# Value products moved beside the next half's scores, two-bank PSUM tiles, the norm without GpSimd arithmetic, y transposes in pairs

## The chip, the cores and the metric

The kernel runs on one core of one Trainium2 chip. The metric is the device time of one launch in microseconds, the median of three runs. A core has a tensor engine (PE, with its weight loads shown as PEld), a vector engine (DVE), a scalar engine (ACT), a GpSimd engine (POOL) and a sync engine (SP) that issues most loads. Each executes its own instructions in order; between engines there are semaphores.

## The reference, cut to what matters

One layer for 256 prompt frames and 64 sample frames (320 columns in all, `T`), model width 2048:

```python
h = rmsnorm(x, norm_pre[l])
proj = jnp.einsum('bsd,de->bse', h, w_in[l])          # 2048 x 15392 weights
# four mixers: A stick-breaking, B chunk-band, C differential, D latent (low rank KV, rotary key)
gated = outs * jax.nn.silu(gate_in)
y_branch = jnp.einsum('bsnc,ncd->bsnd', gated, w_branch[l])
y = jnp.einsum('bsd,de->bse', jnp.sum(sigmoid(merge_in) * y_branch, axis=2), w_out[l])
x = x + rmsnorm(y, norm_post[l])
```

Each mixer is scores (q times k), a softmax or stick-breaking weight, and value products (weights times v). Keys, values and the latent cache are outputs too.

## The kernel before

All weight products keep features on the partitions and the 320 frames in the columns. A weight block of 1024 columns of SBUF is a **unit** (512 KB as a rule). A unit is loaded by SP into `raw` (4 buffers), split into a high part `whi` on ACT (L190) and a low part `wlo` on DVE (L191), 4 buffers each, and multiplied in three products per 128x128 block (L195 to L197: hi by hi, hi by lo, lo by hi). A unit has 24 products of 320 columns; four units in a row make a group that accumulates in a PSUM tile `pm` of two banks. There are two `pm` tiles by turns; the one not in use is `spare_pm()`. The main loop (L1240 on) walks over the units. One turn of it is a **slot**: it emits the load of unit i+3, the split of unit i+3, then background work, then the products of unit i.

**The start.** Units 0 to 7 are the D input projection (`d_units`, products on L910), each of two 128-row chunks k of x. For each k, `first_split` emits on ACT the cast `xhi` (L1177) and the cast `whi` (L175), on DVE `xlo` (L1180) and `wlo` (L178). Between them the table `early` places the norm's squares and sums: of the first four chunks on POOL (L1188), of the rest on ACT (L1184), with the folding sums on POOL in slot 1 (L1192) and on DVE in slots 5 and 6 (L1192). POOL also scales the rotary key weights `wkr` (L1195). Ahead of the last chunk, k=15, `x_rms` needs the folded sum: six tiny products (L1201). After k=15, `krope_mm` runs 32 products of 32 array columns (L789), four side by side.

**The attention.** The heads are cut into eight halves, in the order A0, D0, D1, A1, B0, B1, C0, C1. Each half is two generators (p=0 and p=1) run in step by `pair`; `heavy` runs one half at a time from slot 33 on. A generator yields the number of slots to wait, and with a second number says that it needs the spare `pm` tile. Its stages in fp32 on PE are the scores (L496, L513; D: L489, L490, L510; A: L602, L606, L607), the transposes of the weights (L458 to L460; C: L540 to L544) or A's running sums (L644 to L647), and the value products `pv64` (L409; C: L549 to L552). p=0 takes the spare `pm` tile for scores and transposes, p=1 takes three one-bank tiles from `att()` (four buffers in all). `v_prep`, a light generator two slots after the value group, transposes v (L700, L704), and ACT copies it out (L706, L707).

**The end.** For each of seven groups of the output projection, `out_post` scales the block into `yg`, and a light generator one slot later transposes it (L1073, L1077) and ACT copies it out.

Of the kernel before, what the change touches and what calls it, by code (L numbers as in the profile page):

```python
# [16 lines left out]
D = 2048  # L17
# [45 lines left out]
def hybrid_streaming_kernel(ctx, tc, ins, outs):  # L63
# [44 lines left out]
    def spare_pm():  # L108

        return psm.tile([128, 2, 512], F32, name="sp", tag=f"pm{turn[0] ^ 1}", bufs=1)  # L110

    def att():
        return psa.tile([128, 512], F32, name="att", tag="att", bufs=4)

# [7 lines left out]
    wkr = ppool.tile([128, KC, 32], F32, name="wkr")  # L122
    nrm = cpool.tile([128, 24], F32, name="nrm")
    npost = nrm[:, 0:16]
# [119 lines left out]

    def pair(*gens):

        live = [dict(gen=g, due=0, bar=None) for g in gens]
        while live:  # L250
            go = True
            while go:
                go = False
                for e in list(live):
                    if e["bar"] is None and e["due"] <= slot[0]:
                        try:
                            w = next(e["gen"])
                        except StopIteration:
                            live.remove(e)
# [3 lines left out]
                if live and all(e["bar"] and e["due"] <= slot[0] for e in live):  # L263
                    if live[0]["bar"][1] and not spare_ok(live[0]["bar"][1]):
                        break
                    for e in live:
                        e["bar"] = None
                    go = True
            if live:
                yield 1  # L270

# [3 lines left out]

    light, heavy = Queue(), Queue()

# [3 lines left out]
    def run_background():  # L281
        for e in list(later):
            if e[0] <= slot[0]:
                later.remove(e)
                e[1]()
        step(light)
        if slot[0] >= M["last_q"]:
            step(heavy, 1)

# [156 lines left out]
    def transposes_pt(z, p):  # L446
        p1 = R["p1"]
        zt = p1.tile([128, 1024], F32, name="zt", tag="t1", bufs=2)
        if p == 0:
            sp = spare_pm()  # L450
            tps = [sp[:, 0], sp[:, 1]]
            ts = sp[:, :, 384:512]
# [12 lines left out]

    def attn_softmax(kind, n, hf, p, q, k, v, bias_heads=None):
# [4 lines left out]
        if bias_heads is not None:  # L471
            bp, bsamp = load_bias(bias_heads)
            bias = [bp[:, 0], bp[:, 1 if len(bias_heads) > 1 else 0]]
        else:
            bias = [R["mdz"]] * 2
            bsamp = R["mdz"][:, 0:192]
        z = p1.tile([128, 1024], F32, name="z", tag="t0", bufs=2)
        mx = p1.tile([128, 16], F32, name="mx", tag="mx", bufs=4)
        st = p1.tile([128, 16], F32, name="st", tag="st", bufs=4)
        yield 0, 1 if kind == "C" else 2  # L480
        if p == 0:
            sp = spare_pm()
            S = [sp[:, 0], sp[:, 1]]
        else:
            S = [att(), att()]
        if kind == "D":
# [12 lines left out]

        if p == 0:  # L500
            SSp, zs, cuts = sp[:, :, 384:480], z[:, 768:960].rearrange("p (a c) -> p a c", a=2), 2
            bsamp = bsamp.rearrange("p (a c) -> p a c", a=2)
        else:
            SSp, zs, cuts = att()[:, 0:192], z[:, 768:960], 1
        for c in range(cuts):
            n_k = 192 // cuts
            to, kc = SSp[:, c] if cuts > 1 else SSp, slice(256 + c * n_k, 256 + c * n_k + n_k)
            if kind == "D":
# [9 lines left out]
        if kind != "C":  # L518
# [26 lines left out]
        copy_on(1, zt[:, 768:1024], tp[:, 0:256])  # L545
        yield 2, 0
        o = att()
# [38 lines left out]
    def attn_stick(n, hf, p, q, k, v):  # L586
        p1 = R["p1"]
        t0 = p1.tile([128, 1024], F32, name="a0", tag="t0", bufs=2)
        t1 = p1.tile([128, 1024], F32, name="a1", tag="t1", bufs=2)
        t2 = p1.tile([128, 1024], F32, name="a2", tag="t2", bufs=2)  # L590
        yield 0, 2
        if p == 0:
            sp = spare_pm()
            S = [sp[:, 0], sp[:, 1], sp[:, :, 384:512]]
        else:
            S = [att(), att(), None]

# [5 lines left out]
        yield 0, 0  # L603
        if p:
            S[2] = att()[:, 0:256].rearrange("p (a c) -> p a c", a=2)
        nc.tensor.matmul(S[2][:, 0], k[:, p, 256:384], qblk(q, p), start=True, stop=True)  # L606
# [46 lines left out]
        mask(t1)  # L653
        yield 2, 0
        both = t1[:, 0:512].rearrange("p (b j c) -> p j b c", b=2, j=2)
# [4 lines left out]
    def half_branch(kind, n, hf, col):  # L660
# [23 lines left out]
        def post_v(ps):  # L684
# [6 lines left out]
            nc.gpsimd.dma_start(v[:, 2, :], CV[kind][:, hf * 256:hf * 256 + 256])  # L691
            light.append(v_prep(vt))

        def v_prep(vt):
            v = H["v"]
            yield 2
            tp = att()
# [16 lines left out]
            defer(store)  # L714
            if kind == "A":
# [125 lines left out]
    def q_unit(u0):  # L841
# [34 lines left out]
        def post_nope():  # L876
            ps, g = box["ps"], u0 - 1
            q = M["q", g]
            for j in range(2):
                nc.scalar.activation(q[0:64, j:4:2, :], ps[64 * j:64 * j + 64, :, :T], AF.Copy)  # L880
            heavy.append(pair(*(attn_softmax("D", 3, g, p % 2, q, M["k", p], M["v", g])
                                for p in (2 * g, 2 * g + 1))))

# [168 lines left out]
    def out_post(e, n):  # L1052

        def post(ps):
# [13 lines left out]

            def tr():
                for t in range(2):  # L1070
                    tp = att()
                    for i in range(n):
                        nc.tensor.transpose(tp[:, i * 128:(i + 1) * 128], yg[:, i, t * 128:(t + 1) * 128], ident)  # L1073
                    nc.scalar.activation(E["y"][:, t, e * 128:(e + n) * 128], tp[:, 0:n * 128], AF.Copy)
                tp = att()
# [3 lines left out]
                nc.scalar.activation(E["ys"][r:r + 64, c * 128:(c + n) * 128], tp[0:64, 0:n * 128], AF.Copy)  # L1079
            def gen():  # L1080
                yield
                tr()
            light.append(gen())
        return post
# [86 lines left out]
    for i in range(NRAW):  # L1171
        first_load(i)

    TN = ((0, 128), (1, 128), (2, 64))
# [10 lines left out]

    def x_square_pool(c):
        x = xf[:, 4 * c:4 * c + 4, :T]
        nc.gpsimd.tensor_tensor(xsq[:, 4 * c:4 * c + 4, :], x, x, op=OP.mult)  # L1188

    def x_sum(a, n, c, on=nc.vector):  # L1190

        on.tensor_tensor(xsq[:, a:a + n, :], xsq[:, a:a + n, :], xsq[:, c:c + n, :], op=OP.add)  # L1192
# [14 lines left out]
    def x_rbc():  # L1207
        tp = M["rms"][:, 64:64 + T]
        for t, n in TN:
# [33 lines left out]
    for i, u in enumerate(units):  # L1243
# [7 lines left out]
        if i + AHEAD < FIRST:  # L1251
            first_split(i + AHEAD)
            if i == 0:
                first_load(FIRST - 1)
                nc.sync.dma_start(cp, ins["cp"])
                nc.sync.dma_start(wkr, ins["w_kr"])
                nc.sync.dma_start(nrm, ins["nrm"])
        elif i + AHEAD < len(units):
# [69 lines left out]
```

## Time and profile before

| | us |
|---|---|
| median of three runs | 1176.95 (1176.75 to 1177.08) |
| the profiled execution | 1178.38 |
| its span | 1176.5 |
| PE busy | 1166.4 |
| DVE busy | 613.7 |
| ACT busy | 502.4 |
| POOL busy | 70.4 |

The profiled execution is 1.43 above the median, and 1.88 of its time lies outside the span. Line 4 of the page gives the chain of work that ended last: PE 96% of the span, of which L195 to L197 are 88 points. In views of PE a product's start-to-start distance is its cost; the duration printed for it is longer, since products are pipelined. A row with "xN" merges N products; an fp32 product is recorded as two, a transpose as one.

### The profile page before, as it was taken

To read this page: it belongs to the slowest core of one execution; us is meant where nothing else is said; L and a number is where in the kernel's file an instruction comes from. 1 tells how busy PE (TensorE), PEld (TensorE's weight loads), DVE (VectorE), ACT (ScalarE), POOL (GpSimd) and SP (SyncE) were. 2 spreads that over 40 slices of the span, in tenths; PEclk is the share of its full clock that TensorE was granted. 3 is DMA by queue.
4 is the path that set the end of the run, shared out by engine and by line. 5 is a ranking of instruction groups with operands and counts; after the bars stand their busy time and mean duration, and the time that the engine had idled before them with its cause. 6 is when DMAs were issued, how large, how long until landed. Compare 5 with 4: busy or idle time off the path is not lost.

```text
span 1176.5 us, 19590 instructions
## 1 busy us (share of the span) xinstructions
PE 1166.4 (99%) x8139; PEld 1150.9 (98%) x8139; DVE 613.7 (52%) x849; ACT 502.4 (43%) x723; POOL 70.4 (6%) x129
## 2 busy tenths in 40 slices
PE   9999999999999999999999999999999999999997
PEld 8899999999999999999999999999999999999997
DVE  8565375555754545657444454454444454444444
ACT  7344663446444456535333333333333333334442
POOL 3311100002022010000000000000000000020000
PEclk9999999999999999999999999999999999999999
DMA  8755545445455554545554555555555555566442
GB/s 283 241 183 165 147 130 160 137 137 160 139 151 151 163 153 119 161 144 144 151 155 143 154 144 151 156 149 144 160 145 144 161 144 147 158 193 188 144 125 90
DMA packets 171512, 182.71 MB, mean 155 GB/s; under 512 B 7132, under 2 KB 165200, under 8 KB 171008
## 3 DMA queue, kind: packets, MB, share of 16 engines
q1 hardware_dynamic: 167552, 172.97, 50.1%
q0 software_dynamic: 2656, 5.32, 1.7%
q10 hardware_dynamic: 1216, 3.18, 0.8%
q8 instruction: 64, 1.05, 0.4%
q14 instruction: 24, 0.20, 0.0%
HBM read 174.56 MB, written 9.39 MB: 156 GB/s over the span
## 4 chain that ended last, share of the span: by engine, by line
PE 96%; DVE 1%; DMA 1%; ACT 1%; issue 0%; SPq 0%; DVEq 0%
PE pm L195 30%; PE pm L196 29%; PE pm L197 29%; PE att L409 1%; DMA raw<-in_w_in 1%; PE pm L1108 0%; DVE wlo L178 0%; PE pm L1110 0%; PE pm L1109 0%; PE att L644 0%; PE sp L496 0%; PE att L1073 0%; DVE xsq L1192 0%; DVE xlo L1180 0%; PE att L789 0%
## 5 line engine op out<-in xcount | busy, mean ns | idle before, releaser
L191 DVE TENSOR_TENSOR wlo<-raw,whi 128x1024 fp32r<-128x1024 f32 x301 | 365.6, 1220 | 450.4 <-ACT whi L190 448.5
L195 PE MATMUL pm<-xhi,whi 128*128 128x320 f32 x1856 | 577.5, 311 | 0.0
L197 PE MATMUL pm<-xhi,wlo 128*128 128x320 f32 x1856 | 574.1, 309 | 0.0
L196 PE MATMUL pm<-xlo,whi 128*128 128x320 f32 x1856 | 574.0, 309 | 0.0
L190 ACT ACTIVATE whi<-raw 128x1024 fp32r<-128x1024 f32 x301 | 314.7, 1052 | 410.1 <-PE pm L196 330.2
L195 PEld LDWEIGHTS pm<-xhi,whi 128*128 128x128 f32 x1856 | 348.6, 188 | 2.3 <-issue 1.7
L196 PEld LDWEIGHTS pm<-xlo,whi 128*128 128x128 f32 x1856 | 348.6, 188 | 0.2
L197 PEld LDWEIGHTS pm<-xhi,wlo 128*128 128x128 f32 x1856 | 348.5, 188 | 0.0
L197 PE MATMUL pm<-ghi,wlo 128*128 128x320 f32 x256 | 79.2, 309 | 0.0
L196 PE MATMUL pm<-glo,whi 128*128 128x320 f32 x256 | 79.2, 309 | 0.0
L195 PE MATMUL pm<-ghi,whi 128*128 128x320 f32 x256 | 79.2, 309 | 0.0
L962 ACT ACTIVATE sg<-sg 128x640 f32<-128x640 f32 x32 | 23.6, 738 | 112.4 <-DVE sg L151 112.4
L195 PE MATMUL pm<-yhi,whi 128*128 128x320 f32 x224 | 69.8, 312 | 0.0
L197 PE MATMUL pm<-yhi,wlo 128*128 128x320 f32 x224 | 69.3, 309 | 0.0
L196 PE MATMUL pm<-ylo,whi 128*128 128x320 f32 x224 | 69.2, 309 | 0.0
L151 DVE TENSOR_TENSOR sg<-pm,rbc 128x640 f32<-128x640 f32 x40 | 32.9, 823 | 44.5 <-PE pm L197 44.5
L196 PEld LDWEIGHTS pm<-glo,whi 128*128 128x128 f32 x256 | 48.1, 188 | 0.0
L195 PEld LDWEIGHTS pm<-ghi,whi 128*128 128x128 f32 x256 | 48.1, 188 | 0.0
L197 PEld LDWEIGHTS pm<-ghi,wlo 128*128 128x128 f32 x256 | 48.1, 188 | 0.0
L196 PEld LDWEIGHTS pm<-ylo,whi 128*128 128x128 f32 x224 | 42.1, 188 | 0.0
L195 PEld LDWEIGHTS pm<-yhi,whi 128*128 128x128 f32 x224 | 42.1, 188 | 0.0
L197 PEld LDWEIGHTS pm<-yhi,wlo 128*128 128x128 f32 x224 | 42.1, 188 | 0.0
(337 smaller groups left out, 889.1 us busy)
## 6 DMA issues: line engine op xcount, KB each, us to landing
raw<-in_w_in SPq DMA_DIRECT2D x237, 512.0 KB, 3.8
raw<-in_w_branch SPq DMA_DIRECT2D x32, 512.0 KB, 3.6
raw<-in_w_out SPq DMA_DIRECT2D x32, 512.0 KB, 3.8
xrp<-in_x_prompt SPq DMA_DIRECT2D x1, 2048.0 KB, 8.4
out_xp<-ytp SPq DMA_DIRECT2D x8, 256.0 KB, 2.1
xf<-in_x_t SPq DMA_DIRECT2D x5, 321.0 KB, 6.3
scr<-in_bb ACTq DMA_DIRECT2D x1, 1536.0 KB, 9.1
bp<-scr POOLq DMA_DIRECT2D x12, 128.0 KB, 2.4
```

The source lines that it names most:

```text
L151: nc.vector.tensor_tensor(out, ps, rb(n, i, rows, cols), op=OP.mult)
L190: nc.scalar.activation(h, raw, AF.Copy)
L191: nc.vector.tensor_tensor(l, raw, h.bitcast(F32), op=OP.subtract)
L195: nc.tensor.matmul(out, wh, xh, start=first, stop=False)
L196: nc.tensor.matmul(out, wh, xl, start=False, stop=False)
L197: nc.tensor.matmul(out, wl, xh, start=False, stop=last)
L409: nc.tensor.matmul(o[64 * j:64 * j + 64, a:b], v[:, blk, vc + 64 * j:vc + 64 * j + 64], z[j][blk], start=first, stop=not first)
L962: nc.scalar.activation(s, s, AF.Sigmoid)
```

## The change

- `att2()` gives a PSUM tile of two banks (two buffers); `att()` hands out halves of such a tile. p=1 takes an `att2()` tile with p=0's layout: one tile for scores and transposes, the sample scores in two products of 96 columns where p=1 had one of 192.
- `pair` becomes the class `Pair`. Up to two halves run at once. A half that stands before its value products ("pv") waits until the next half stands before its scores ("qk"); then one slot holds the next half's `v_prep`, the earlier half's value products and the next half's scores. After 10 slots of waiting, and for C1, the value products go alone. `v_prep` is no light generator any more, except for A0.
- The squares of x are all on ACT (slots 1, 3, 4, 5), the sums all on DVE (slots 3 to 6). `wkr` is scaled on DVE in slot 2, by 16 columns that `nrm` now carries; `nrm` and `wkr` are loaded behind the loads of unit 3, not behind those of unit 7.
- The y transposes of two groups are done in one slot, and those of the two prompt blocks share one copy.

```diff
+    def att2():
+        half.clear()
+        return psa.tile([128, 2, 512], F32, name="att", tag="att", bufs=2)
     def att():
-        return psa.tile([128, 512], F32, name="att", tag="att", bufs=4)
+        if not half:
+            t = att2()
+            half.extend((t[:, 1], t[:, 0]))
+        return half.pop()
...
+    WAIT = 10
+    class Pair:
+        def run(self, before=None):
+            if before and not before.scored:
+                return
...
+                    if self.at("pv") and not (self.joined or self.last or
+                                              slot[0] - max(e["due"] for e in self.live) >= WAIT):
+                        return
+                    if self.at("qk"):
+                        if before and not (before.at("pv") or before.joined or before.through):
+                            return
+                        if self.front:
+                            self.front()
+                        if before and before.at("pv"):
+                            before.joined = True
+                            before.run()
+                        self.scored = True
...
         if slot[0] >= M["last_q"]:
-            step(heavy, 1)
+            for h in range(min(2, len(heavy))):
+                heavy[h].run(heavy[0] if h else None)
+            while heavy and heavy[0].through:
+                heavy.pop(0)
...
     def transposes_pt(z, p):
-        if p == 0:
-            sp = spare_pm()
...
-        else:
-            tps = [att(), att()]
-            ts = att()[:, 0:256].rearrange("p (a c) -> p a c", a=2)
+        sp = att2() if p else spare_pm()
+        tps = [sp[:, 0], sp[:, 1]]
+        ts = sp[:, :, 384:512]
...
+        yield 0, 1 if kind == "C" else 2, "qk"
...
-        yield 0, 1 if kind == "C" else 2
-        if p == 0:
-            sp = spare_pm()
-            S = [sp[:, 0], sp[:, 1]]
-        else:
-            S = [att(), att()]
+        sp = att2() if p else spare_pm()
+        S = [sp[:, 0], sp[:, 1]]
...
-            SSp, zs, cuts = att()[:, 0:192], z[:, 768:960], 1
...
+        for c in range(2):
+            to, kc = SSp[:, c], slice(256 + c * 96, 352 + c * 96)
...
-            yield 2, 0
+            yield 2, 0, "pv"
             pv64(...)
...
-            light.append(v_prep(vt))
+            if kind == "A" and hf == 0:
+                light.append(v_early(vt))
+            else:
+                attend(3, lambda: v_prep(vt))
...
-            heavy.append(pair(*gens))
+            heavy.append(Pair(gens, front, after, kind == "C" and hf == 1))
...
             def tr():
+                tp = att().rearrange("p (t c) -> p t c", t=2)
                 for t in range(2):
-                    tp = att()
...
-            light.append(gen())
+            E.setdefault("tr", []).append(tr)
+            if len(E["tr"]) == 2 or e == 12:
+                light.append(gen(E.pop("tr")))
...
     for i in range(NRAW):
         first_load(i)
+    nc.sync.dma_start(nrm, ins["nrm"])
+    nc.sync.dma_start(wkr, ins["w_kr"])
...
     def kr_scale():
-        nc.gpsimd.tensor_tensor(wkr, wkr, xf[:, :, T:T + 1].to_broadcast([128, KC, 32]), op=OP.mult)
+        nc.vector.tensor_tensor(wkr, wkr, nrm[:, 24:40].rearrange("p (k o) -> p k o", o=1).to_broadcast([128, KC, 32]),
+                                op=OP.mult)
...
-    early = {0: [lambda: x_square_pool(0)],
-             1: [lambda: x_square(1)] + [lambda n=n: x_sum(0, n, n, nc.gpsimd) for n in (4, 2, 1)],
-             3: [lambda: x_square(2)],
-             5: [lambda: x_square(3), lambda: x_sum(8, 4, 12)],
-             6: [lambda: x_sum(8, 2, 10), lambda: x_sum(8, 1, 9), lambda: x_sum(0, 1, 8)]}
-    early[4] = [kr_scale]
+    early = {1: [lambda: x_square(0)],
+             2: [kr_scale],
+             3: [lambda: x_square(1), lambda: x_sum(0, 4, 4)],
+             4: [lambda: x_square(2), lambda: x_sum(0, 4, 8)],
+             5: [lambda: x_square(3), lambda: x_sum(0, 4, 12)],
+             6: [lambda: x_sum(0, 2, 2), lambda: x_sum(0, 1, 1)]}
```

## Rows read from the trace of the kernel before

**Rows 1.** The page, part 1: busy us (share of the span) and instructions.

```profile
PE 1166.4 (99%) x8139; PEld 1150.9 (98%) x8139; DVE 613.7 (52%) x849; ACT 502.4 (43%) x723; POOL 70.4 (6%) x129
```

**Rows 2.** Waits of PE, whole run: us in total, times, longest.

```profile
PE pm L910 <- DVE wlo L178: 1.2, 1, 1.2
PE att L1201 <- DVE xsq L1192: 1.1, 1, 1.1
```

**Rows 3.** Timeline of PE at 9 us: start us, duration us, instruction, [idle before, releaser].

```profile
8.76 0.31 PE L910 MATMUL pm<-xhi,whi 128*128 128x320 f32 x1
8.91 0.31 PE L910 MATMUL pm<-xlo,whi 128*128 128x320 f32 x1
10.38 0.41 PE L910 MATMUL pm<-xhi,wlo 128*128 128x320 f32 x1 [1.16 <-DVE wlo L178]
```

**Rows 4.** Timeline of DVE in the first 35 us.

```profile
7.54 2.78 DVE L178 TENSOR_TENSOR wlo<-raw,whi 128x512 fp32r<-128x512 f32 x1
10.25 0.54 DVE L1180 SCALAR_TENSOR_TENSOR xlo<-xf,xhi 128x320 fp32r<-128x320 f32 x1
10.71 0.68 DVE L178 TENSOR_TENSOR wlo<-raw,whi 128x512 fp32r<-128x512 f32 x1
...
16.01 3.00 DVE L1180 SCALAR_TENSOR_TENSOR xlo<-xf,xhi 128x320 fp32r<-128x320 f32 x1 [0.37 <-ACT xhi L1177]
...
29.88 1.48 DVE L1192 TENSOR_TENSOR xsq<-xsq 128x1280 f32<-128x1280 f32 x1
...
32.42 1.93 DVE L1192 TENSOR_TENSOR xsq<-xsq 128x640 f32<-128x640 f32 x3
```

**Rows 5.** Timeline of POOL in the first 35 us.

```profile
7.45 2.33 POOL L1188 TENSOR_TENSOR xsq<-xf 128x1280 f32<-128x1280 f32 x1 [6.47 <-DMA xf<-in_x_t]
15.68 6.05 POOL L1192 TENSOR_TENSOR xsq<-xsq 128x1280 f32<-128x1280 f32 x3 [5.90 <-ACT xsq L1184]
```

**Rows 6.** Timeline of PE at the norm, 34 to 37 us.

```profile
34.40 0.81 PE L1201 MATMUL att<-ones,xsq 128*128 128x2 f32 x6 [1.06 <-DVE xsq L1192]
...
36.12 0.47 PE L910 MATMUL att<-xhi,whi 128*128 128x320 f32 x1
36.39 0.47 PE L910 MATMUL att<-xlo,whi 128*128 128x320 f32 x1
```

**Rows 7.** Line L789 in two windows: us, PE, PEld busy (count), PEclk, DMA.

```profile
37.85:39.45 1.60, 1.59 (x12) 0.59 (x16) 0.50 0.94 229
39.45:40.95 1.50, 1.50 (x24) 0.51 (x16) 0.98 0.76 257
```

**Rows 8.** Timeline of PE, slot 79: v transposes and value products in one block.

```profile
320.93 0.60 PE L700 MATMUL att<-cp,vt 128*128 128x128 f32 x4
321.36 0.38 PE L704 MATMUL att<-cp,vt 128*64 128x128 f32 x2
321.67 1.99 PE L409 MATMUL att<-a,v 128*64 128x256 f32 x32
323.59 0.42 PE L195 MATMUL pm<-xhi,whi 128*128 128x320 f32 x1
323.84 0.31 PE L196 MATMUL pm<-xlo,whi 128*128 128x320 f32 x1
```

**Rows 9.** Timeline of PE, slot 82: the scores of B0 in a block of their own.

```profile
334.11 0.31 PE L197 MATMUL pm<-xhi,wlo 128*128 128x320 f32 x1
334.35 0.93 PE L496 MATMUL sp<-k,q 64*128 64x128 f32 x8
...
335.86 0.69 PE L513 MATMUL sp<-k,q 128*128 128x96 f32 x4
336.38 0.52 PE L513 MATMUL att<-k,q 128*128 128x192 f32 x2
336.60 0.44 PE L195 MATMUL pm<-xhi,whi 128*128 128x320 f32 x1
```

**Rows 10.** Timeline of ACT beside the block of slot 79.

```profile
322.65 0.46 ACT L707 ACTIVATE v<-att,rstat 64x256 f32<-64x256 f32 x1
```

More of the change, by code (lines that the diff above doesn't have):

```diff
@@ L110, in spare_pm @@
         return psm.tile([128, 2, 512], F32, name="sp", tag=f"pm{turn[0] ^ 1}", bufs=1)
+    half = []
+    def att2():
+        half.clear()
+        return psa.tile([128, 2, 512], F32, name="att", tag="att", bufs=2)
     def att():
-        return psa.tile([128, 512], F32, name="att", tag="att", bufs=4)
+        if not half:
+            t = att2()
+            half.extend((t[:, 1], t[:, 0]))
+        return half.pop()
     ppool_ctx = ExitStack()
@@ L122, in hybrid_streaming_kernel @@
     wkr = ppool.tile([128, KC, 32], F32, name="wkr")
-    nrm = cpool.tile([128, 24], F32, name="nrm")
+    nrm = cpool.tile([128, 40], F32, name="nrm")
     npost = nrm[:, 0:16]
@@ L243, in spare_ok, with __init__, at @@
         return slot[0] >= len(units) or 0 < units[slot[0]].get("left", 0) <= most
-    def pair(*gens):
-        live = [dict(gen=g, due=0, bar=None) for g in gens]
-        while live:
+    WAIT = 10
+    class Pair:
+        def __init__(self, gens, front=None, after=0, last=False):
+            self.live = [dict(gen=g, due=slot[0] + after, bar=None) for g in gens]
+            self.front, self.last, self.scored, self.joined = front, last, False, False
+        def at(self, stage):
+            return all(e["bar"] and e["due"] <= slot[0] and e["bar"][2:] == (stage,) for e in self.live)
+        def run(self, before=None):
+            if before and not before.scored:
+                return
             go = True
@@ L253, in pair @@
                 go = False
-                for e in list(live):
+                for e in list(self.live):
                     if e["bar"] is None and e["due"] <= slot[0]:
@@ L258, in pair @@
                         except StopIteration:
-                            live.remove(e)
+                            self.live.remove(e)
                             continue
@@ L262, in pair, with through @@
                         e["due"] = slot[0] + w
[L263 to L266, printed above, removed]
+                if self.live and all(e["bar"] and e["due"] <= slot[0] for e in self.live):
+                    if self.live[0]["bar"][1] and not spare_ok(self.live[0]["bar"][1]):
+                        return
[4 more added lines that the diff above has]
+                        if before and not (before.at("pv") or before.joined or before.through):
+                            return
+                        if self.front:
[4 more added lines that the diff above has]
+                        self.scored = True
+                    if self.at("pv"):
+                        self.joined = True
+                    for e in self.live:
                         e["bar"] = None
                     go = True
-            if live:
-                yield 1
+        @property
+        def through(self):
+            return not self.live
     class Queue(list):
@@ L274, in append @@
             super().append([g, 0])
-    light, heavy = Queue(), Queue()
+    light, heavy = Queue(), []
     def defer(fn, n=2):
@@ L498, in attn_softmax @@
         yield 0, 0
[L500 to L503, printed above, removed]
-            SSp, zs, cuts = att()[:, 0:192], z[:, 768:960], 1
-        for c in range(cuts):
-            n_k = 192 // cuts
-            to, kc = SSp[:, c] if cuts > 1 else SSp, slice(256 + c * n_k, 256 + c * n_k + n_k)
+        SSp, zs = sp[:, :, 384:480], z[:, 768:960].rearrange("p (a c) -> p a c", a=2)
+        bsamp = bsamp.rearrange("p (a c) -> p a c", a=2)
+        for c in range(2):
+            to, kc = SSp[:, c], slice(256 + c * 96, 352 + c * 96)
             if kind == "D":
@@ L545, in attn_softmax @@
         copy_on(1, zt[:, 768:1024], tp[:, 0:256])
-        yield 2, 0
+        yield 2, 0, "pv"
         o = att()
@@ L587, in attn_stick @@
         p1 = R["p1"]
+        yield 0, 2, "qk"
         t0 = p1.tile([128, 1024], F32, name="a0", tag="t0", bufs=2)
@@ L590, in attn_stick @@
         t2 = p1.tile([128, 1024], F32, name="a2", tag="t2", bufs=2)
[L591 to L596, printed above, removed]
+        sp = att2() if p else spare_pm()
+        S = [sp[:, 0], sp[:, 1], sp[:, :, 384:512]]
         for kb, a, b in ((0, 0, 256), (128, 256, 384)):
@@ L603, in attn_stick @@
         yield 0, 0
-        if p:
-            S[2] = att()[:, 0:256].rearrange("p (a c) -> p a c", a=2)
         nc.tensor.matmul(S[2][:, 0], k[:, p, 256:384], qblk(q, p), start=True, stop=True)
@@ L653, in attn_stick @@
         mask(t1)
-        yield 2, 0
+        yield 2, 0, "pv"
         both = t1[:, 0:512].rearrange("p (b j c) -> p j b c", b=2, j=2)
@@ L691, in post_v, with v_early @@
             nc.gpsimd.dma_start(v[:, 2, :], CV[kind][:, hf * 256:hf * 256 + 256])
-            light.append(v_prep(vt))
+            if kind == "A" and hf == 0:
+                light.append(v_early(vt))
+            else:
+                attend(3, lambda: v_prep(vt))
+        def v_early(vt):
+            yield 2
+            v_prep(vt)
+            attend(1, None)
         def v_prep(vt):
             v = H["v"]
-            yield 2
             tp = att()
@@ L714, in v_prep, with attend @@
             defer(store)
+        def attend(after, front):
+            v = H["v"]
             if kind == "A":
@@ L880, in post_nope @@
                 nc.scalar.activation(q[0:64, j:4:2, :], ps[64 * j:64 * j + 64, :, :T], AF.Copy)
-            heavy.append(pair(*(attn_softmax("D", 3, g, p % 2, q, M["k", p], M["v", g])
-                                for p in (2 * g, 2 * g + 1))))
+            heavy.append(Pair([attn_softmax("D", 3, g, p % 2, q, M["k", p], M["v", g])
+                               for p in (2 * g, 2 * g + 1)], after=1))
         units.append(dict(src=w_qup[:, u0 * 256:(u0 + 1) * 256], kn=3, cols=256, mm=mm,
@@ L1069, in tr @@
             def tr():
+                tp = att().rearrange("p (t c) -> p t c", t=2)
                 for t in range(2):
-                    tp = att()
                     for i in range(n):
-                        nc.tensor.transpose(tp[:, i * 128:(i + 1) * 128], yg[:, i, t * 128:(t + 1) * 128], ident)
-                    nc.scalar.activation(E["y"][:, t, e * 128:(e + n) * 128], tp[:, 0:n * 128], AF.Copy)
+                        nc.tensor.transpose(tp[:, t, i * 128:(i + 1) * 128], yg[:, i, t * 128:(t + 1) * 128], ident)
+                nc.scalar.activation(E["y"][:, :, e * 128:(e + n) * 128], tp[:, :, 0:n * 128], AF.Copy)
                 tp = att()
@@ L1079, in tr, with gen @@
                 nc.scalar.activation(E["ys"][r:r + 64, c * 128:(c + n) * 128], tp[0:64, 0:n * 128], AF.Copy)
-            def gen():
+            def gen(trs):
                 yield
-                tr()
-            light.append(gen())
+                for f in trs:
+                    f()
+            E.setdefault("tr", []).append(tr)
+            if len(E["tr"]) == 2 or e == 12:
+                light.append(gen(E.pop("tr")))
         return post
@@ L1184, in x_square, with x_sum @@
         nc.scalar.activation(xsq[:, 4 * c:4 * c + 4, :], xf[:, 4 * c:4 * c + 4, :T], AF.Square)
[L1186 to L1192, printed above, removed]
+    def x_sum(a, n, c):
+        nc.vector.tensor_tensor(xsq[:, a:a + n, :], xsq[:, a:a + n, :], xsq[:, c:c + n, :], op=OP.add)
     def kr_scale():
-        nc.gpsimd.tensor_tensor(wkr, wkr, xf[:, :, T:T + 1].to_broadcast([128, KC, 32]), op=OP.mult)
+        nc.vector.tensor_tensor(wkr, wkr, nrm[:, 24:40].rearrange("p (k o) -> p k o", o=1).to_broadcast([128, KC, 32]),
+                                op=OP.mult)
     def x_rms():
@@ L1255, in hybrid_streaming_kernel @@
                 nc.sync.dma_start(cp, ins["cp"])
-                nc.sync.dma_start(wkr, ins["w_kr"])
-                nc.sync.dma_start(nrm, ins["nrm"])
         elif i + AHEAD < len(units):
@@ L1296 @@
                                                                "diff_subln")]
-    arrays["nrm"] = np.zeros((128, 24), np.float32)
+    arrays["nrm"] = np.zeros((128, 40), np.float32)
+    arrays["nrm"][:, 24:40] = np.asarray(inputs["norm_pre"])[0].reshape(KC, 128).T
     arrays["nrm"][:, 0:21] = np.concatenate(vecs).T
```

2 lines of the change are left out of this document (removed).

## The prediction

> **What bounds the kernel now.** I read the page's busy times first: PE is busy for 1166.4 of 1176.5 us [rows 1]. So only two things can move the time by much: a wait of PE, or the number and cost of what PE executes. The list of PE's waits comes next. Beside the wait for the first constant at the very start it has two entries, 1.2 us on a weight split and 1.1 us on the norm's sum [rows 2]. In the whole attention and in the last two thirds of the run PE waits for nobody. The third view is PE's timeline at these two places, the fourth that of DVE and POOL beside them, and the last are three fp32 blocks in the attention, where the reader is to see what it costs PE to go from one kind of product to another.
>
> **The start, where the gain should be.** At 8.91 us PE issues a product and the next one only at 10.38 [rows 3]. The distance just before is 0.15 [rows 3], the usual one for 320 columns, so 1.32 us are lost. The releaser is a `wlo` on DVE that took 2.78 us, where one of the same shape takes 0.68 [rows 4]. POOL's square ran from 7.45 to 9.78 just then [rows 5], and the `wlo` ended 0.5 us behind it. The same shows again at 16 us: an `xlo` takes 3.00 instead of 0.54 [rows 4] while POOL sums [rows 5]. So an arithmetic instruction of POOL holds up the two-input instructions of DVE for its whole length. POOL's four are 8.4 us long; the change removes them, and POOL's `wkr` scaling too.
>
> Without POOL the `wlo` for k=2 starts at 7.54 and ends near 8.2, before PE wants it at 9.06. For the later chunks PE comes 1.3 us earlier than before, and ACT, which casts ahead of DVE, is not touched by POOL; I find no chunk whose cast ends later than 1.8 us before PE's need. The first loss goes: **1.32 us**.
>
> Then the norm. Without the first loss PE reaches `x_rms` at about 31.86 (33.18 before, 1.22 ahead of 34.40 as below). When is the sum there? DVE takes the chunk k=8 up at 16.0, when ACT has cast it [rows 4]. From there its queue holds eight chunks of `xlo` and `wlo` at 0.46 + 0.60 (start to start; the printed 0.54 and 0.68 overlap by 0.08 [rows 4]) = 8.5; `wkr` at the price of a `wlo` of equal size, 0.6; three sums of 1280 columns at 1.48 less 0.08 [rows 4] = 4.2; one split of 1024 columns, 1.15 (twice 0.60 less an overhead); two small sums, about 1.3 of the 1.93 that three took [rows 4]. Sum 15.75, so the end is near 31.75 and PE waits 0 to 0.3 us, where it lost 1.22 (1.06 idle [rows 6] and the 0.16 by which the two measures differ at the first stall). I take 0.15 for what is left: **1.07 us** gained. The sums come to DVE, and with `wkr` they cost it 2.8 us more than before (6.1 against 1.4 and 1.93), but it gets back most of POOL's 8.4.
>
> Third, the clock. Behind the wait at 34.40 PE's products go from a pitch of 0.15 to 0.27 at 36.12 [rows 6], and the granted clock is 0.50 until 39.45 [rows 7]: the 1.2 GHz level. It is the one place in the trace where this happens. Ahead of it PE had waited 1.06 us and then done six tiny products [rows 6]; after the first stall at 9 us, with full products on both sides, the clock stayed at 2.4 GHz. Without the wait I expect no drop. It cost six products at 0.12 more, 0.72, and half of the first window of L789, 1.60 at clock 0.50 [rows 7], 0.80. Together **1.5 us**.
>
> Added at the start: `nrm` and `wkr` go into SP's queue ahead of four units' loads, two issues and 268 KB, under 1 us for each load behind them. I estimate that PE's need of unit 4 still comes over 2 us behind its split, as ACT takes up unit 4 in order, behind units 2 and 3, and not at once when it lands. In DVE's queue, `wkr`'s scaling now waits for a load with the splits of units 5 to 7 behind it, but stands at about 18 us with PE's first need behind it near 22. I price both at nothing; if that cover is gone, it is the second rival below.
>
> **The attention.** Following the yields slot by slot, there are seven joins: A0 with D0's scores, D0 with D1, D1 with A1, A1 with B0, B0 with B1, B1 with C0, C0 with C1. Five of them have a `v_prep` in front. The attention ends four slots earlier, 13 slots before phase 2 opens, and that costs or gives nothing.
>
> What does PE save in a join? The products are the same. Going into value products on half the array costs 0.09 (a start 0.24 after the last product [rows 9], not 0.15), coming out 0.11 (0.25 [rows 8]). Where `v_prep` and value products already stood in one block, the two last transposes took 0.31, where four took 0.43 [rows 8]: the 0.09 is paid inside the block. So the join with `v_prep` saves nothing. The join of value products and scores takes out one coming-out and one going-in, 0.20, where both use part of the array: D1/A1, A1/B0, B0/B1, B1/C0. The D scores and C's value products use the whole array and save nothing. Below, the saving is nil, as at the `v_prep`; above, it may reach 0.4, as blocks also lose something at their inner ends that merged rows don't show. I take 0.2, four times: 0.8 gained.
>
> Against it, p=1's sample scores in B and C become two products of 96 columns. The two records of the 192-column product last 0.22 up to the next start, four of 96 columns take 0.52 with 0.09 of going over [rows 9], 0.43 without; the first large product behind them starts its successor after 0.28 [rows 9], against 0.25 after other blocks [rows 8], so some comes back. Between 0 and 0.2 a half, I take 0.1, four times: 0.4 lost. D's are priced at nothing. The net of the attention is **0.4 us** (minus 0.8 to plus 1.6).
>
> The Trainium skill (TensorEngine Tiling (Array Packing), Key Properties) says that a change of tiling mode drains the engine. Value products on column halves and scores on row halves are two modes, so by that rule a join still holds three changes where two blocks held four. By it the four joins would save one change each, about 0.1 to 0.2, hence 0.4 to 0.8 in all; no row here shows such a change directly.
>
> The y transposes: whole-array transposes, twelve in a block instead of twice six. I price that at nothing (at most three goings-in and comings-out, 0.6). One ACT copy less per group is off the path. The last group stays alone, so the tail is as it was.
>
> **The sum.** 1.32 + 1.07 + 1.5 + 0.4 = 4.3 us. The profiled execution takes 1178.38, so it would take 1174.1; the median of the runs is 1.43 below that execution, hence 1176.95 - 4.3 = **1172.6 us**.
>
> **The rivals.**
> - *The clock falls all the same.* The six tiny products and then `krope_mm`, with a quarter of the array each, stand together still. Against it: during the second half of L789 the clock was back at 0.98 [rows 7]. Gain 2.8, time 1174.2.
> - *The sum is late again.* The margin at `x_rms` is nil by my own sum; one late load (`wkr`, or unit 8, which ACT now reaches with one more square behind it) or one more DVE wait of 1 us brings back the stall and with it the clock drop. Gain 1.32 + 0.4 = 1.7, time 1175.2.
> - *The first stall only changes hands:* with DVE fast, PE waits for a load there. The loads run at full rate in that stretch. Gain 3.0, time 1174.0.
> - *Slower: two-bank tiles make PE wait.* In the five joins with a front, p=1's scores need the tile that `v_prep` has just used, so PE must wait for ACT's three copies, with the 24 products of the slot behind it. In slot 79 the copies end at 323.11 [rows 10], the value products at 323.59 [rows 8], and p=0's scores need another 0.76 (half of the 1.51 of both) [rows 9]: 1.24 us in hand. It decides once ACT is over 1.24 late; to make the kernel slower by 2.4, ACT would have to be late by 2.6 five times. At 3 us late the price is 5 x 1.76 = 8.8, time 1181.4. Against it: joins lie seven slots or more apart, and ACT's long run of exponentials falls behind a join, not ahead of one.
>
> **How the numbers follow.** This kernel can be told from no change by about 0.2%, 2.35 us. Forecast 0.62; clock falls 0.14; sum late 0.11; first stall changes hands 0.06; two-bank waits 0.07. Faster by over 0.2% (below 1174.6) hold the forecast, the first and the third: 0.82; within 0.2% the late sum: 0.11; slower 0.07. The range: below, all terms at their best, 1.32 + 1.22 + 1.5 + 1.6 + 0.6 = 6.2, gives 1170.8; above it takes in the late sum with a little, 1175.4. It is kept that wide, with more than 8 in 10 inside by my cases, because the margin at `x_rms` is nil. Outside is the two-bank case.
>
> **What would show it.** In PE's waits: no `wlo` at 9 us, and at `x_rms` at most 0.3. In DVE's timeline: `wlo` of 512 columns at 0.68 throughout the first 30 us. Granted clock 1.00 at the norm. Seven blocks with value products and scores in one, 0.2 shorter than the two apart; no wait of PE on `att` in them. The forecast is wrong if the wait at `x_rms` is near 1 us again, if the clock drops behind it, or if PE waits on ACT's L706 or L707.

## The result and the profile after

The changed kernel takes 1215.34 us (1211.98 to 1219.65, four runs), the kernel before 1177.01 beside it: ratio 1.0325, interval 1.0309 to 1.0342. The forecast was 1172.6 in a range up to 1175.4. The kernel became 38 us slower.

The page's busy times of the changed kernel, which answer to [rows 1] (span 1212.8 us, execution 1214.6 us; its mean granted clock is 0.992):

```profile
PE 1176.9 (97%) x8155; PEld 1158.9 (96%) x8155; DVE 611.3 (50%) x851; ACT 504.7 (42%) x718; POOL 60.7 (5%) x124
```

PE has hardly more work, but is no longer busy for 99% of the span. The list of PE's waits, which answers to [rows 2] (us in total, times, longest):

```profile
PE att L1112 <- ACT ytp L1109: 7.6, 7, 2.4
PE att L450 <- DVE gate L459: 5.4, 4, 1.8
PE att L595 <- ACT oc L596: 4.6, 2, 2.3
PE att L573 <- ACT zt L423: 3.4, 4, 1.1
PE att L604 <- DVE kvd L784: 2.9, 1, 2.9
PE att L579 <- DVE oc L585: 2.2, 2, 1.3
PE att L450 <- ACT gate L461: 1.5, 2, 0.8
PE sp L145 <- POOL ones L142: 1.0, 1, 1.0
PE att L833 <- ACT rs L605: 0.7, 1, 0.7
```

The two waits of [rows 2] are gone. In their place stand 23 others, 28.3 us of idle time without the one for `ones`, which the kernel before had too. All have the output `att`. They are in the attention, in D's norms, in C's norms and at the y transposes, but none is on a read of a `v_prep` product.

What they have in common is seen at the first value products. The timeline from 186 us, all engines, lines of the same slot:

```profile
186.11 1.06 ACT L199 ACTIVATE whi<-raw 128x1024 fp32r<-128x1024 f32 x1 [2.41 <-PE pm L205]
...
186.15 1.10 PE L450 MATMUL att<-a,v 128*64 128x256 f32 x16
187.20 1.22 DVE L200 TENSOR_TENSOR wlo<-raw,whi 128x1024 fp32r<-128x1024 f32 x1 [2.24 <-ACT whi L199]
188.45 0.49 DVE L459 TENSOR_TENSOR gate<-att,gate 128x320 f32<-128x320 f32 x1
...
189.00 1.10 PE L450 MATMUL att<-a,v 128*64 128x256 f32 x16 [1.75 <-DVE gate L459]
```

Before, the value products of both generators were one unbroken row of 32 records, as L409 in [rows 8]. Now p=0's 16 records write one half of a two-bank tile and p=1's the other half; between the two stands, in program order, the `put` of p=0 (L459), which reads the first half. p=1's products start only when that read has ended. The read is in DVE's queue behind a `wlo` of 1.22 us, and that behind ACT's `whi`. So PE waits for two engines' queues, for data that its product doesn't touch. The y transposes show the same with ACT (L1112 behind the copy on L1109):

```profile
1104.67 0.60 PE L1108 MATMUL att<-cp,yg 128*128 128x128 f32 x4
1106.31 0.41 PE L1112 MATMUL att<-cp,yg 128*64 128x128 f32 x2 [1.05 <-ACT ytp L1109]
```

The waits are in the program: its list of PE instructions has a wait on the Activation semaphore at the first product of L1112, where the kernel before has none at L1077 of the first group.

Five stretches with work on PE also show a lower granted clock (columns: us, PE, PEld, DVE, ACT, POOL busy, PEclk, DMA share, GB/s):

```profile
57.50:61.50 4.00, 4.00 (x19) 4.00 (x20) 0.88 (x3) 0.72 (x3) 0.00 (x0) 0.57 0.79 232
466.50:470.50 4.00, 3.23 (x10) 2.84 (x11) 3.46 (x3) 1.17 (x4) 0.00 (x0) 0.61 0.88 243
505.00:509.00 4.00, 4.00 (x19) 4.00 (x18) 3.01 (x3) 0.89 (x2) 0.00 (x0) 0.59 0.35 120
1139.00:1143.00 4.00, 3.56 (x15) 3.56 (x16) 0.00 (x0) 0.76 (x2) 0.00 (x0) 0.60 0.59 193
1187.00:1191.00 4.00, 2.89 (x14) 2.86 (x15) 1.23 (x1) 1.43 (x3) 0.00 (x0) 0.57 0.00 0
```

Most of each stretch shown is at the 1.2 GHz level. Each stands at one or more of the waits of the list: behind them in the first four, and in the last from within the wait of 2.4 us that ends at 1188.1.

The start is as forecast. A line of DVE's timeline, which answers to [rows 4], and then PE's at the norm, which answer to [rows 6]:

```profile
8.08 0.69 DVE L187 TENSOR_TENSOR wlo<-raw,whi 128x512 fp32r<-128x512 f32 x1 [0.20 <-ACT whi L184]
```

```profile
32.02 0.31 PE L945 MATMUL att<-xhi,wlo 128*128 128x320 f32 x1
32.17 0.79 PE L1238 MATMUL att<-ones,xsq 128*128 128x2 f32 x6
32.88 0.42 PE L945 MATMUL pm<-xhi,whi 128*128 128x320 f32 x1
```

The `wlo` takes 0.69 where it took 2.78 beside POOL's square, and the norm's six products follow at the usual distance of 0.15.

### The profile page after: what moved, and what is told of

The parts are those of the page before. It is cut to its first block, busy times and chain, and to the rows that moved or that the text cites. A ratio compares the mean times of both kernels' runs of the same rounds, so it can differ in the third digit from the quotient of the medians.

```text
span 1212.8 us, 19609 instructions
## 1 busy us (share of the span) xinstructions
PE 1176.9 (97%) x8155; PEld 1158.9 (96%) x8155; DVE 611.3 (50%) x851; ACT 504.7 (42%) x718; POOL 60.7 (5%) x124
## 3 DMA queue, kind: packets, MB, share of 16 engines
q8 instruction: 64, 1.05, 0.4%
## 4 chain that ended last, share of the span: by engine, by line
PE 95%; ACT 3%; DVE 1%; issue 1%; DVEq 0%; POOL 0%; ACTq 0%; POOLq 0%
PE pm L204 29%; PE pm L205 29%; PE pm L206 28%; ACT whi L199 1%; PE pm L945 1%; PE att L945 1%; DVE wlo L200 1%; PE att L450 1%; PE pm L1146 0%; PE pm L1147 0%; PE pm L1148 0%; PE att L669 0%; PE sp L145 0%; ACT ytp L1109 0%; PE sp L530 0%
```

## The experiments

**Theory A**: with two halves in one tile, a product into one half waits for every read of the other half that stands ahead of it in the program. **Rivals**: the joined blocks crowd DVE and ACT so that their reads come late; or two large tiles give less room than four small ones; or the start delays what follows.

**e1: the change with one-bank tiles.** All of the change, but `att()` and p=1's layout are those of before.

```diff
-    def att2():
-        half.clear()
-        return psa.tile([128, 2, 512], F32, name="att", tag="att", bufs=2)
     def att():
-        if not half:
-            t = att2()
-            half.extend((t[:, 1], t[:, 0]))
-        return half.pop()
+        return psa.tile([128, 512], F32, name="att", tag="att", bufs=4)
```

> The changed kernel with four one-bank att tiles and p=1's old three-tile layout; joins, start and paired y transposes stay. Theory A (a product into one half of a two-bank tile waits for the reads of the other half that stand ahead of it in the program): no wait of PE on att is left, 1172.6 us (1171.5 to 1174). Rival B (the joins crowd DVE and ACT, and PE waits for their copies whatever the tiles are): the waits stay, over 1195 us.

Measured: 1175.20 us (1174.79 to 1177.71, ten runs), ratio 0.9986 (0.9976 to 0.9995). Its waits of PE are only:

```profile
PE sp L136 <- POOL ones L133: 1.0, 1, 1.0
PE att L572 <- DVE z L565: 0.8, 2, 0.4
```

So 40.1 us of the changed kernel hang on the tiles and p=1's layout in them, and the joins and the start are not their cause. But 1175.20 is 2.6 above what was expected; e3 and e5 say where those are.

**e2: the tiles alone.** The kernel before with `att2()` and p=1's new layout, no join, no new start.

```diff
-        return psa.tile([128, 512], F32, name="att", tag="att", bufs=4)
+        if not half:
+            t = att2()
+            half.extend((t[:, 1], t[:, 0]))
+        return half.pop()
```

> The kernel before with the two-bank tiles and p=1's new layout alone. Theory A: the same kind of waits in every pair of value products, in C, in the norms and at the y transposes, some 25 us of idle PE and clock drops behind the long ones, 1205 to 1220 us. Rival B: no joins, so no crowding, 1176 to 1180 us.

Measured: 1220.25 us (1217.68 to 1222.03, four runs), ratio 1.0362 (1.0346 to 1.0377). The longest of its waits are the same kinds as above:

```profile
PE att L418 <- DVE gate L427: 6.8, 4, 2.4
PE att L1066 <- ACT ytp L1067: 5.6, 4, 2.4
PE att L563 <- ACT oc L564: 4.6, 2, 2.3
```

Without any join the loss is there in full: crowding by the joins falls.

**e4: the tiles kept, all products ahead of the first read.** The whole change, with the emission order altered in four places: the reads of p=0's value products (`put`, in C the copies into `oc`) after p=1's value products, both of C's transposes ahead of the copies, C's norm products ahead of the first square root, the y transposes of all three blocks ahead of the copies. The sharing of tiles in D's norms is left.

```diff
-            pv64([(both[:, j], ...)
+            o = pv64([(both[:, j], ...)
+            yield 0, 0
+            put(n, 2 * hf + p, o)
...
+                ts = att()
+                for i in range(n):
+                    nc.tensor.transpose(ts[0:64, i * 128:(i + 1) * 128], yg[:, i, 256:320], ident)
                 nc.scalar.activation(E["y"][:, :, e * 128:(e + n) * 128], tp[:, :, 0:n * 128], AF.Copy)
-                tp = att()
-                for i in range(n):
-                    nc.tensor.transpose(tp[0:64, i * 128:(i + 1) * 128], yg[:, i, 256:320], ident)
```

> The changed kernel with its two-bank tiles, but all products into both halves of a tile are emitted ahead of the first read of either half: value products, C's transposes, C's norm, y transposes. The two waits in the D norms (0.65 and 2.9 us idle) are left as they are. Theory A: only these two waits are left, with one clock drop, 1176 to 1179 us. Rival C (two tiles in turn are too few where four stood, whatever the order): most of the waits stay, over 1195 us.

Measured: 1181.84 us (1180.49 to 1183.91, four runs), ratio 1.0043 (1.0026 to 1.006). The waits left:

```profile
PE att L611 <- DVE kvd L793: 2.9, 1, 2.9
PE sp L145 <- POOL ones L142: 1.0, 1, 1.0
PE att L572 <- DVE z L565: 0.7, 2, 0.4
PE att L842 <- ACT rs L612: 0.7, 1, 0.7
```

The tiles are the same and equally few; with the order alone, 33.5 us come back. What is left of the sharing is D's norms (2.9 and 0.7), and the granted clock from 57.5 to 61.5 us is 0.57 here too. The time is 2.8 above the upper end of what was expected; e1 too lies 2.6 above its forecast.

**e3: the new start alone**, on the kernel before: squares on ACT, sums and `wkr` on DVE, `nrm` and `wkr` loaded early.

> The kernel before with the squares on ACT, sums and the scaling of wkr on DVE and the two early loads, nothing else. The prediction's terms for the start: 1.32 + 1.07 + 1.5 = 3.9 us less, 1173.1 us (1172.5 to 1174). Rival (the first stall only changes hands or the clock falls all the same): 1174 to 1176 us.

Measured: 1174.88 us (1174.33 to 1177.67, ten runs), ratio 0.9979 (0.997 to 0.9988): a gain of 2.4, where 3.9 were forecast. 2.4 is the sum of the two stalls, 1.32 and 1.07; the 1.5 for the clock don't come. In its profiled execution the sum was late once more, behind a `whi` on ACT that had waited 1.58 us at 19.6 (first line ACT, second PE's wait):

```profile
19.57 0.63 ACT L175 ACTIVATE whi<-raw 128x512 fp32r<-128x512 f32 x1 [1.58 <-PE att L910]
```

```profile
PE att L1200 <- DVE xsq L1190: 1.4, 1, 1.4
```

How many of the other nine executions had this wait isn't known, so the agreement of the 2.4 to a tenth is partly luck.

**e5: the joins alone**, on the kernel before, with one-bank tiles.

> The kernel before with the joins alone: one-bank tiles, the old start, y transposes one by one. The look with one-bank tiles showed 0.2 us saved in each of four joins and a new wait of PE on DVE at C1's transposes that costs 1.27 us, since C0's norm now stands in DVE's queue ahead of C1's weights. So 0.5 us more than before, 1177.5 us (1177 to 1178). The prediction's 0.8 us gained in the joins, without that wait, would give 1176.4.

Measured: 1177.64 us (1177.3 to 1178.15, ten runs) against 1177.12 (22 runs), ratio 1.0003 (0.9994 to 1.0012). The medians are 0.5 apart, as expected, but that is not clear of the noise; the rows have to show it. The join of A1 and B0 in PE's timeline answers to [rows 8] and [rows 9] together:

```profile
304.54 0.60 PE L739 MATMUL att<-cp,vt 128*128 128x128 f32 x4
304.98 0.38 PE L743 MATMUL att<-cp,vt 128*64 128x128 f32 x2
305.29 1.99 PE L441 MATMUL att<-a,v 128*64 128x256 f32 x32
307.20 0.93 PE L528 MATMUL sp<-k,q 64*128 64x128 f32 x8
...
309.24 0.52 PE L545 MATMUL att<-k,q 128*128 128x192 f32 x2
309.45 0.44 PE L195 MATMUL pm<-xhi,whi 128*128 128x320 f32 x1
```

From the first transpose to the first large product behind, 4.91 us; apart they took 2.66 [rows 8] and 2.25 [rows 9], 4.91 too. But outside of them one going-in (0.09) and one coming-out (0.10) are no longer paid: 0.2 saved, as forecast. Taken as the distance that a block puts between the large products around it, each of the four joins is 0.2 shorter than its parts in the kernel before. Four of these are 0.8. Against it stands a wait that the forecast didn't have. PE at 459 us and DVE a little earlier, in e1, where it is the same:

```profile
459.15 0.27 PE L576 MATMUL att<-cp,z 128*128 128x128 f32 x1
459.81 0.30 PE L572 MATMUL att<-cp,z 128*128 128x128 f32 x1 [0.39 <-DVE z L565]
460.50 0.44 PE L572 MATMUL att<-cp,z 128*128 128x128 f32 x2 [0.39 <-DVE z L565]
```

```profile
450.20 2.15 DVE L599 RECIPROCAL oc<-oc 128x320 f32<-128x320 f32 x1
...
453.89 2.15 DVE L599 RECIPROCAL oc<-oc 128x320 f32<-128x320 f32 x1 [0.95 <-ACT oc L598]
```

C1's scores now stand in the same slot as C0's value products, so C0's norm, with two reciprocals of 2.15 us, falls ahead of C1's scaling of `z` in DVE's queue. C1's transposes come too soon: the ten take 1.27 us more than before (2.36 against 1.10, each time less the usual distance of the large products around them).

**e6: the sample's y transposes in a tile of their own.** The changed kernel, one word altered:

```diff
-                tp = att()
+                tp = att2()[:, 0]
```

> The changed kernel, where in the y transposes alone the sample block gets a two-bank tile of its own instead of the second half of the prompt blocks' tile. Theory A: the seven waits at this place (7.6 us idle) go, and with them the two clock drops behind them; all others stay: 1201 to 1206 us in one look. Rival C (too few tiles in turn): the waits stay or grow, since more tiles are asked for.

Measured: 1210.16 us, one execution. The seven waits on L1112 (7.6 us) are gone, but at the group's next transposes, and at the last norm, there are new ones:

```profile
PE att L1108 <- ACT ytp L1109: 2.5, 3, 0.8
PE att L1129 <- ACT ytp L1109: 0.8, 1, 0.8
```

That is the other price of large tiles: with two buffers, the second group's products need the tile that the first group's copy has not yet freed. So 4.3 of the 7.6 came back, and the time is above the 1201 to 1206 expected. As the changed kernel's own runs span 7.7 us, this single execution says little on time; the list of waits is what counts.

**e8: the new start with `nrm` and `wkr` loaded as late as before**, `wkr` scaled in slot 7.

> The start alone, with nrm and wkr loaded where they were before and wkr scaled in slot 7, behind the sums: 0.6 us less in DVE's queue ahead of the norm, and no load ahead of units 4 to 7. If the 1.36 us wait at the norm in the look at the start alone came from a load of unit 5 that landed late behind these two, it goes: 1174.3 us (1174 to 1174.7), and fewer runs above 1175. If not, 1174.9 as there.

Measured: 1174.66 us (1174.07 to 1177.32, eleven runs), ratio 0.9979 (0.9971 to 0.9988). Between this and e3's 1174.88 there is no difference to be told: four of eleven runs lie above 1175, where e3 has five of ten. Its profiled execution has no wait at the norm, but a new one of 0.2 for a `wlo` at 7.5 us. What the late loads are worth stays open.

**e9: what is left when the losses go.** e1 with the start of e8 and C's transposes one slot later:

```diff
-        yield 3, 0
+        yield 4, 0
         zt = p1.tile([128, 1024], F32, name="zt", tag="t1", bufs=2)
```

> One-bank tiles, joins, paired y transposes, the start with wkr late, and C's transposes one slot later, so that DVE has C1's weights done. Against the one-bank kernel (1175.2) the 1.27 us at C1 go and the norm has its margin: 1173.7 us (1173.2 to 1174.3). If C1's wait is not DVE's queue but a later consequence of the join, 1175.

Measured: 1173.80 us (1173.49 to 1175.02, six runs), ratio 0.9969 (0.9957 to 0.9981). It is 41.5 below the changed kernel and 3.3 below the kernel before. The wait on `z` is gone. Against e1 the time is 1.4 less, near the 1.27 of that wait; the start is another too, so the two are not parted. Its profiled execution, the slowest of the six, has one wait of 0.9 at the norm.

**e7: POOL's square put back.** The start of e3, but the first square on POOL as before.

> The kernel with the new start alone, but the square of the first 1280 columns of x goes back to GpSimd in slot 0; the other squares and all sums stay where the new start has them. It tells apart who held DVE at 7.5 us in the kernel before. Theory A (an arithmetic instruction of GpSimd holds DVE's two-input instructions for its length): the wlo that falls beside it takes 2.5 to 3.0 us instead of 0.68 and ends about 0.5 us behind GpSimd's square, and PE waits 1.1 to 1.5 us for it at about 9 us; the time is 1.3 us above that of the start alone, 1176.2. Rival (the wlo was slow because its data or its neighbours were late, or because of the sums): the wlo stays near 0.7, no wait at 9 us, 1174.9.

Measured: 1175.45 us, one execution. POOL, DVE and PE:

```profile
7.69 2.32 POOL L1220 TENSOR_TENSOR xsq<-xf 128x1280 f32<-128x1280 f32 x1 [6.71 <-DMA xf<-in_x_t]
```

```profile
7.70 2.85 DVE L178 TENSOR_TENSOR wlo<-raw,whi 128x512 fp32r<-128x512 f32 x1
```

```profile
PE pm L910 <- DVE wlo L178: 1.1, 1, 1.1
```

One POOL instruction of 2.32 us, put back alone, stretches the `wlo` beside it from 0.69 to 2.85 and brings PE's stall back. The time rose by only 0.6 against e3's median, less than the 1.3 expected; this execution had no wait at the norm, where e3's profiled one had 1.4, and one execution can't part the two.

**e10: D's norms too get tiles of their own.** e4, with `att2()[:, 0]` for the products of `rnorm_front`, `rnorm_back` and `krope`.

> The kernel of 'products first' (all of the change, the two-bank tiles kept, every product into both halves of a tile ahead of the first read), and now the two norms of D and k's rope also stop sharing tiles: each of their products gets a two-bank tile to itself. There 2.9 and 0.7 us of PE's waits were left, with a fall of the granted clock behind them. Theory A (what the two-bank tiles cost is only the waits between halves, and what follows from them): no wait of PE on kvd and none on rs; granted clock 1.00 from 57.5 to 61.5 us; the time falls by 2.9 + 0.7 + 1.7 for the clock and a few tenths, to 1176.3, within 1.2 of the one-bank version's 1175.20; the two waits on z since 0.8 in all stay. Rival B (half as many tiles, though larger, cost by themselves, as products wait for the tile used two before): waits of PE on another reader come up in the same places, and the time stays above 1178. Rival C (the fall of the clock at 57 us has nothing to do with the wait ahead of it): the waits go, the clock still falls, 1178.

Measured: 1176.06 us (1174.96 to 1178.34, ten runs), ratio 0.9994 (0.9984 to 1.0003). Waits and clock:

```profile
PE att L1247 <- DVE xsq L1237: 1.7, 1, 1.7
PE sp L145 <- POOL ones L142: 1.0, 1, 1.0
PE att L572 <- DVE z L565: 0.7, 2, 0.4
```

```profile
34.00:42.00 8.00, 8.00 (x71) 6.19 (x71) 5.25 (x9) 1.90 (x4) 2.84 (x8) 1.00 0.85 263
...
57.50:61.50 4.00, 4.00 (x29) 4.00 (x28) 2.04 (x5) 1.46 (x4) 0.00 (x0) 1.00 0.55 156
```

With two-bank tiles and no wait between halves left, the kernel is within 0.9 us of the one-bank version e1, and about half of that would be the two sample products of p=1 (below). The fall of the clock at 57 us went with the wait of 2.9 us ahead of it. Other than that the tiles cost nothing that can be seen here.

## Why the prediction was wrong

**Which step failed: the price of `att()`.** The prediction costed the two-bank tiles only where p=1's scores would take over the tile of `v_prep`, and put 0.07 on that rival with 1181.4. That place is harmless: no wait on those copies in the list of waits. So the rival had the right direction and the wrong wait. The change's second half, that `att()` now hands out halves of one tile to all its other users, was given no price at all, neither in the sum nor in the bounds. The runs showed 23 waits there with 28.3 us of idle time, and 40.1 us in all against e1. There the unit that is waited for grew from one bank to two. The diff shows it: two `att()` in a row, with a read of the first between them, stand in `rnorm`, in `pv64` by p, in C's transposes and in `tr`. In the kernel before they got different tiles and no wait.

**How 28.3 us of waits become 39.6.** The spans of the changed kernel and of e1 are 1212.8 and 1173.2. The waits account for 28.3 - 0.8 = 27.5. With each wait PE loses more than the idle time printed: at 1104.67, four transposes at 0.11 would have brought the next at 1105.11, and it came at 1106.31, 1.20 later with 1.05 printed. Taken over whole blocks against the same blocks without a wait in e1 and e4, it is 0.1 to 0.3 a wait, 0.2 as a rule (the block at 186 is 1.96 longer with 1.75 printed); 21 waits more make some 4. And the five stretches at a lower clock cost up to 4 us times (0.43 + 0.39 + 0.41 + 0.40 + 0.43) = 8.2, or 7.3 if only the time counts in which PE was busy. With 0.5 for the sample products of p=1 (below) that is 39 to 40, an estimate, against 39.6.

**The banks** themselves do not call for the wait. In e1 each bank is a tile, and there is none: ACT copies y transposes out of one bank from 1077.83 to 1078.41, and PE transposes into another at 1077.90. In e2 two banks are a tile and there are waits. The Trainium skill (PSUM — Partial Sum Buffer, Summary: rules for kernel authors) asks to guard PSUM by bank, and to read another bank than the one being written. By that rule p=1's products, in the other bank, need no wait, and e1 agrees. The kernels with large tiles keep to a coarser unit, the tile. The wait stands in the instruction stream, so it was laid down when the kernel was built; a two-bank tile with the wait left out wasn't tried.

**The first stall, 1.32, and the norm, 1.07: right.** No `wlo` wait at 9 us, 0.69 throughout, no wait at `x_rms` in the changed kernel and in e1; e3 gains 2.4. e7 shows that POOL's arithmetic is what held DVE. The Trainium skill (SBUF — State Buffer, Terms) says of the port pair that DVE and GpSimd share that the loser is blocked for the whole instruction; the `wlo` of 2.85 beside 2.32 on POOL agrees. The margin at `x_rms` was called nil, and so it was: waits of 1.4 in e3, 0.9 in e9 and 1.7 in e10, none in e1 and e8. In the three with a wait ACT had stood still for 0.9 to 1.6 us ahead of a `whi` near 19.7, in e10 for its load; what e3 and e9 waited for there is not settled. (The two early loads are 276 KB, not 268, as `nrm` grew to 20 KB; no wait shows that it mattered.)

**The clock, 1.5: the wrong base.** The fall behind the norm [rows 7] was in the profiled execution of before, but the term was taken from the median. Of the 54 executions of the kernel before that stood beside the timed runs (e7 aside), eight list a mean clock of 0.997 and take 1178.2 to 1179.2; the others list 0.998 or 0.999 and take 1176.6 to 1178.1. The profiled one, 1178.38, is like the eight, and the 1.43 that I carried over as a fixed distance to the median is nearly the 1.5 of this fall. And a wait there need not bring it on: behind 1.7 us of waiting in e10 the clock stayed at 1.00 up to 42 us, and with the old start behind 0.9 in e5 too. Nor does the new start end such executions: one of ten in e1 and in e3, one of eleven in e8 and three of ten in e10 list 0.997 and take 1177.3 to 1178.3. Where their fall lies was not profiled. (The fall was also not the only one in the trace: from 1174 us on the clock is at 0.50, but there PE has no more work.)

**The attention, 0.4: its terms were right, one was missing.** A join saved 0.2 in the four where it was forecast, and nothing at A0/D0, D0/D1 and C0/C1. (The Trainium skill, TensorEngine Tiling (Array Packing), Key Properties: a change of mode drains the engine. By it one change fewer in a join was to save 0.1 to 0.2, an estimate, and the 0.2 of e5 agrees.) Two products of 96 columns for one of 192 cost 0.12 a half (B0's and B1's joined blocks take 5.17 in e4 and 5.05 in e1, worked out as the distance that they put between the large products around them), 0.1 taken. The paired y transposes gain nothing: twelve take 1.31, twice six 2 x 0.655. Not in the sum was DVE's order behind the last join, 1.27 lost at C1's transposes; with it the joins come to +0.5 instead of -0.8, and e5's medians agree, within their noise.

The sum without the two-bank tiles is thus 2.4 + 0.8 - 1.27 = 1.9 below 1177.2, 1175.3; e1 measured 1175.20. With the C wait taken out e9 reaches 1173.80, near the forecast of 1172.6 plus the clock's 1.5.

## What to carry to other kernels

When a buffer grows, list every place that takes one, and at each ask which reads now stand between two writes of the same tile: the price is the length of the reading engine's queue, and a tensor engine that was never idle pays it whole. Where two products share a tile, emit both ahead of the first read, or give each a tile, if there are enough buffers (e6 had too few). And a disturbance seen in the one profiled execution is subtracted from that execution, not from the median of others that may not have it.

## What was not expected of the hardware

The granted clock fell to the 1.2 GHz level, for most of the 4 us shown each time, behind some waits of PE and not behind others: behind 2.9 us at 54 us in the changed kernel and in e4, but not behind 1.7 at the norm in e10, while the kernel before had it behind 1.06 in the execution that was profiled. What decides it, no run here shows. With the waits the runs of the changed kernel spread wider too, over 7.7 us in four runs, with mean clocks from 0.995 for the shortest to 0.989 for the longest, where those of before spread over 0.3 in the four beside them and over 2.6 in the 54.
